# Contrast adjustment on one core: 64 KB rows in three buffers, and all transfers on SyncE's queue

## The chip, the cores and the metric

The kernel runs on one core of one Trainium2 chip. The core has a matrix engine (TensorE, PE in the profile), a vector engine (VectorE, DVE), a scalar engine (ScalarE, ACT), GpSimd (POOL) and SyncE (SP), which here only issues transfers. 16 DMA engines move the data between the chip's memory (HBM) and the on-chip buffer with its 128 partitions. Transfers are put into queues by SyncE and by ScalarE; both queues are served by the same 16 DMA engines. The metric is the device time of one execution in microseconds, median of several runs; less is better.

## The reference

```python
x = np.random.rand(16, 3, 512, 512).astype(np.float32)    # 48 planes of 262,144 pixels, 50.3 MB
factor = np.float32(1.5)

mean = np.mean(x, axis=(2, 3), keepdims=True)
return np.clip(mean + factor * (x - mean), 0, 1).astype(np.float32)
```

Every plane needs its mean before one of its pixels can be written. The kernel computes `factor * x + shift` with `shift = (1 - factor) * mean`, and clips the result to 0 and 1. All of `x` is read once and as many bytes are written, 100.66 MB in all.

## The kernel before

A tile is 128 rows of `ROW` = 8192 floats (32 KB), one row to each partition, 4 MB in all. A plane fills 32 rows, so a tile has four planes, and there are 12 tiles. They lie in `ring`, a tile of six buffers; tile `t` uses buffer `t % 6` and is computed in place.

The work on one tile is in `compute` (L81 to L94):

- VectorE sums the first `SUM` = 4352 floats of each row (the `tensor_reduce`, L81), and beside it ScalarE sums the other 3840 (the `activation` with `accum_out`, L84). ScalarE's copy goes to `junk`, which nobody reads.
- Two matrix products (L86 and L87) with `blockw` add the sums over the 32 rows of a plane, multiply by `(1 - factor) / pixels` and give every row its `shift`, in `bias`. The first takes ScalarE's sum, the second VectorE's.
- VectorE multiplies and adds (L91), then clips (L94), over the whole row. Only tile 0 is done in two pieces, 2048 and 6144 floats.
- `store` (L101) writes the result back. It is issued by ScalarE, so it stands in ScalarE's order behind the sum of its own tile and ahead of the sum of the next.

`load` (L76) is issued by SyncE. Before the loop stand five loads: tile 0 in two pieces (1 MB and 3 MB), tile 1, tiles 2 and 3 in one transfer of 8 MB, and tiles 4 and 5 likewise. In the loop, after tile `t`, tile `t + 6` is loaded into the same buffer, so its load waits in SyncE's order until the store of tile `t` has landed. The order of the program is as written (`manual_schedule`); each engine runs its instructions in that order, with semaphores for what depends on another engine. Stores go through ScalarE's queue (q10 in the profile) and loads through SyncE's (q1), so loads and stores can be under way side by side.

`blockw` is set up on GpSimd at the start by five memsets, one over everything (L61) and one for each block (L63).

Of the kernel before, what the change touches and what calls it, by code (L numbers as in the profile page):

```python
# [1 line left out]

# [4 lines left out]


P = 128  # L10
ROW = 8192
BUFS = 6
SHORT = 2048
FIRST = (SHORT, ROW - SHORT)
SUM = 4352


@with_exitstack
def kernel(
    ctx: ExitStack,  # L20
    tc: tile.TileContext,
    x: bass.AP,
    factor: float,
    out: bass.AP,
):

    nc = tc.nc
    f32 = mybir.dt.float32  # L30
    Alu = mybir.AluOpType
    Act = mybir.ActivationFunctionType

    B, C, H, W = x.shape
    n_img, n_pix = B * C, H * W
    ppi = n_pix // ROW
    per_tile = P // ppi
    n_tiles = n_img // per_tile
    assert ppi * ROW == n_pix and per_tile * n_tiles == n_img

    factor = float(factor)
    wconst = (1.0 - factor) / float(n_pix)

    x_f = x.rearrange("b c h w -> (b c h w)")
    out_f = out.rearrange("b c h w -> (b c h w)")

    def dram(ap, t, c0=0, c1=ROW):
        return bass.AP(tensor=ap.tensor, offset=t * P * ROW + c0, ap=[[ROW, P], [1, c1 - c0]])

    consts = ctx.enter_context(tc.tile_pool(name="consts", bufs=1))  # L50
    xpool = ctx.enter_context(tc.tile_pool(name="xpool", bufs=1))
    small = ctx.enter_context(tc.tile_pool(name="small", bufs=1))
    psum = ctx.enter_context(tc.tile_pool(name="psum", bufs=1, space=bass.MemoryType.PSUM))


    sums = small.tile([P, 2 * n_tiles], f32, name="sums")
    junk = small.tile([P, ROW - SUM], f32, name="junk")
    bias = psum.tile([P, n_tiles], f32, name="bias")

    blockw = consts.tile([P, P], f32, name="blockw")  # L60
    nc.gpsimd.memset(blockw, 0.0)  # L61
    for a in range(0, P, ppi):
        nc.gpsimd.memset(blockw[a : a + ppi, a : a + ppi], wconst)  # L63


    ring = xpool.tile([P, BUFS, ROW], f32, name="ring")

    def load(t, c0=0, c1=ROW, n=1):

        b = t % BUFS  # L70
        src = bass.AP(
            tensor=x_f.tensor,
            offset=t * P * ROW + c0,
            ap=[[ROW, P], [P * ROW, n], [1, c1 - c0]],
        )
        nc.sync.dma_start(out=ring[:, b : b + n, c0:c1], in_=src)  # L76

    def compute(t):
        xt = ring[:, t % BUFS, :]
        own = sums[:, 2 * t : 2 * t + 2]  # L80
        nc.vector.tensor_reduce(  # L81
            out=own[:, 0:1], in_=xt[:, 0:SUM], axis=mybir.AxisListType.X, op=Alu.add
        )
        nc.scalar.activation(out=junk, in_=xt[:, SUM:ROW], func=Act.Copy, accum_out=own[:, 1:2])  # L84
        shift = bias[:, t : t + 1]
        nc.tensor.matmul(shift, blockw, own[:, 1:2], start=True, stop=False)  # L86
        nc.tensor.matmul(shift, blockw, own[:, 0:1], start=False, stop=True)  # L87
        c = 0
        for n in FIRST if t == 0 else [ROW]:
            part = xt[:, c : c + n]  # L90
            nc.vector.tensor_scalar(  # L91
                out=part, in0=part, scalar1=factor, scalar2=shift, op0=Alu.mult, op1=Alu.add
            )
            nc.vector.tensor_scalar(  # L94
                out=part, in0=part, scalar1=0.0, scalar2=1.0, op0=Alu.max, op1=Alu.min
            )
            store(t, c, c + n)
            c += n

    def store(t, c0, c1):  # L100
        nc.scalar.dma_start(out=dram(out_f, t, c0, c1), in_=ring[:, t % BUFS, c0:c1])  # L101

    with tc.manual_schedule():
        load(0, c1=SHORT)
        load(0, c0=SHORT)
        load(1)
        load(2, n=2)
        load(4, n=2)
        for t in range(n_tiles):
            compute(t)  # L110
            if t + BUFS < n_tiles:
                load(t + BUFS)


# [1 line left out]
_INS = ['x', 'factor']  # L116
_OUTS = [((16, 3, 512, 512), 'float32')]

_NUMBERS = {'factor': 1.5}


# [26 lines left out]
```

## Time and profile before

| | before |
|---|---|
| median of 3 runs (lowest to highest) | 239.11 us (239.05 to 239.17) |
| span of the profiled execution, first to last instruction | 237.3 us |
| bytes moved, mean rate over the span | 100.66 MB, 424 GB/s |
| VectorE busy | 163.1 us |
| ScalarE busy | 43.2 us |
| TensorE busy | 14.1 us |
| GpSimd busy | 0.9 us |
| packets of all DMA queues | 3712 |

The profile is of one execution, and its own time is known only as this span. The span begins at the first instruction and ends at the last, and the measured time of a run has a little more around it. Shares are shares of the span. A line such as "L81 DVE ..." is a group of instructions from one line of the kernel on one engine, with its count, busy time and mean. "DMA share" is the mean busy share of the 16 DMA engines. A packet is what a DMA engine moves in one go; here it is one row of a transfer, or the semaphore write that closes a transfer on an engine. A packet counts where it starts, so in short windows the rates waver.

### The profile page before, as it was taken

How to read it: one execution, taken by the hardware profiler on the slowest of the kernel's cores; microseconds unless marked ns; L12 is line 12 of the kernel's file. 1: busy time of each engine (PE TensorE's matmuls, PEld its weight loads, DVE VectorE, ACT ScalarE, POOL GpSimd, SP SyncE). 2: the span in 40 equal slices, each digit the busy share in tenths (PEclk: the TensorE clock that was granted, in tenths of full speed). 3: DMA queues.
4: the chain of work that ended last, by engine and by line, in shares of the span. 5: the costliest groups of instructions: out<-in, count | busy, mean ns of one | idle time of the engine just before them, and what ended most of it. 6: DMA issues, size and time to landing. Idle time of an engine off the chain costs nothing.

```text
span 237.3 us, 285 instructions
## 1 busy us (share of the span) xinstructions
PE 14.1 (6%) x48; PEld 12.0 (5%) x48; DVE 163.1 (69%) x38; ACT 43.2 (18%) x25; POOL 0.9 (0%) x9
## 2 busy tenths in 40 slices
PE   0010010001010001010010100100100100010000
PEld 0010010001010001010010100100100100010000
DVE  0079989048989328999989898891892795687000
ACT  2050230041050023050320504101400500500000
POOL 1000000000000000000000000000000000000000
DMA  7999999999999999999999999999999999999996
GB/s 297 410 442 442 421 442 359 456 439 441 442 436 414 403 431 442 442 442 442 436 442 436 414 409 425 442 442 442 442 436 442 436 420 403 425 442 442 442 442 265
DMA packets 3712, 100.66 MB, mean 424 GB/s; under 512 B 384, under 2 KB 384, under 8 KB 384
## 3 DMA queue, kind: packets, MB, share of 16 engines
q1 hardware_dynamic: 1840, 50.33, 49.7%
q10 hardware_dynamic: 1872, 50.33, 49.2%
HBM read 50.33 MB, written 50.33 MB: 424 GB/s over the span
## 4 chain that ended last, share of the span: by engine, by line
DMA 57%; DVE 29%; another core or an unknown queue 3%; PE 1%; SPq 1%; issue 0%; DVEq 0%
DMA ring<-in_x_dram 41%; DMA out_dram<-ring 16%; DVE sums L81 10%; DVE ring L91 9%; DVE ring L94 9%; PE bias L87 1%; SPq L76 1%; DVEq L91 0%
## 5 line engine op out<-in xcount | busy, mean ns | idle before, releaser
L81 DVE TENSOR_REDUCE sums<-ring 128x1 f32<-128x4352 f32 x12 | 56.2, 4683 | 45.7 <-DMA ring<-in_x_dram 45.7
L84 ACT ACTIVATE junk<-ring 128x3840 f32<-128x3840 f32 x12 | 40.8, 3403 | 163.3 <-DMA ring<-in_x_dram 107.5
L91 DVE TENSOR_SCALAR ring<-ring,bias 128x8192 f32<-128x8192 f32 (+2 forms) x13 | 54.1, 4163 | 8.9 <-PE bias L87 7.4
L94 DVE TENSOR_SCALAR ring<-ring 128x8192 f32<-128x8192 f32 (+2 forms) x13 | 53.3, 4099 | 0.4
L86 PE MATMUL bias<-sums,blockw 128*128 128x1 f32 x24 | 7.0, 361 | 190.8 <-ACT junk L84 190.8
L86 PEld LDWEIGHTS bias<-sums,blockw 128*128 128x128 f32 x24 | 6.0, 312 | 191.7 <-ACT junk L84 175.2
L87 PE MATMUL bias<-sums,blockw 128*128 128x1 f32 x24 | 7.0, 363 | 4.3 <-DVE sums L81 3.9
L87 PEld LDWEIGHTS bias<-sums,blockw 128*128 128x128 f32 x24 | 6.0, 311 | 5.3 <-DVE sums L81 5.0
L84 ACT ACTIVATION_READ_ACCUMULATOR junk<-ring 128x1 f32 x12 | 2.2, 186 | 0.0
L84 ACT ACT_TABLE_LOAD x1 | 1.3, 1283 | 0.7 <-PEq L129 0.7
L63 POOL MEMSET blockw<- 32x32 f32 x4 | 0.5, 117 | 0.2
L61 POOL MEMSET blockw<- 128x128 f32 x1 | 0.2, 204 | 0.3 <-POOLq L129 0.3
L129 POOL MEMSET const-bfloat16-1.0<- 128x1 bf16 x1 | 0.1, 111 | 0.0
L129 POOL MEMSET const-uint8-127<- 128x1 uint8 x1 | 0.1, 111 | 0.0
L129 POOL MEMSET const-float32-1.0<- 128x1 f32 x1 | 0.1, 108 | 0.0
L129 POOL MEMSET const-float32-0.0<- 128x1 f32 x1 | 0.1, 103 | 0.2 <-issue 0.2
## 6 DMA issues: line engine op xcount, KB each, us to landing
out_dram<-ring ACTq DMA_DIRECT2D x11, 4096.0 KB, 35.8
ring<-in_x_dram SPq DMA_DIRECT2D x7, 4096.0 KB, 49.7
ring<-in_x_dram SPq DMA_DIRECT2D x2, 8192.0 KB, 66.7
ring<-in_x_dram SPq DMA_DIRECT2D x1, 3072.0 KB, 11.7
out_dram<-ring ACTq DMA_DIRECT2D x1, 3072.0 KB, 28.2
ring<-in_x_dram SPq DMA_DIRECT2D x1, 1024.0 KB, 4.8
out_dram<-ring ACTq DMA_DIRECT2D x1, 1024.0 KB, 17.5
```

Of the source, the lines that this page charges most:

```text
L61: nc.gpsimd.memset(blockw, 0.0)
L63: nc.gpsimd.memset(blockw[a : a + ppi, a : a + ppi], wconst)
L76: nc.sync.dma_start(out=ring[:, b : b + n, c0:c1], in_=src)
L81: nc.vector.tensor_reduce(out=own[:, 0:1], in_=xt[:, 0:SUM], axis=mybir.AxisListType.X, op=Alu.add)
L84: nc.scalar.activation(out=junk, in_=xt[:, SUM:ROW], func=Act.Copy, accum_out=own[:, 1:2])
L86: nc.tensor.matmul(shift, blockw, own[:, 1:2], start=True, stop=False)
L87: nc.tensor.matmul(shift, blockw, own[:, 0:1], start=False, stop=True)
L91: nc.vector.tensor_scalar(out=part, in0=part, scalar1=factor, scalar2=shift, op0=Alu.mult, op1=Alu.add)
L94: nc.vector.tensor_scalar(out=part, in0=part, scalar1=0.0, scalar2=1.0, op0=Alu.max, op1=Alu.min)
L129: nc = _bacc.Bacc("TRN2", target_bir_lowering=False, num_devices=1)
```

## The change

`ROW` becomes 16,384 floats (64 KB), and `ring` has three buffers in place of six, which is the same size. A tile is now 8 MB and eight planes of 16 rows; there are six tiles. For each tile there are now two sums on VectorE and two on ScalarE (one of each for each half of the row), and four matrix products, the last of which takes VectorE's second sum. Multiply-add and clip run over 16,384 floats at a time, except in the last tile, which is done in two halves.

All transfers are issued by SyncE. The order is written out: loads of tile 0 (two pieces, 1 MB and 7 MB), 1 and 2; stores of 0 and 1; loads of 3 and 4; stores of 2 and 3; load of 5 in two halves; stores of 4 and of the two halves of 5. The waits follow from the three buffers: tile 3 takes the buffer of tile 0, tile 4 that of 1, tile 5 that of 2. `blockw` is filled by one memset and cut to its blocks by two `affine_select`.

```diff
-ROW = 8192
-BUFS = 6
+ROW = 16384
+HALF = ROW // 2
+BUFS = 3
 SHORT = 2048
-FIRST = (SHORT, ROW - SHORT)
 SUM = 4352
...
-    nc.gpsimd.memset(blockw, 0.0)
-    for a in range(0, P, ppi):
-        nc.gpsimd.memset(blockw[a : a + ppi, a : a + ppi], wconst)
+    blocks = blockw.rearrange("p (a b) -> p a b", b=ppi)
+    nc.gpsimd.memset(blockw, wconst)
+    for base, step in ((0, -ppi), (ppi - 1, ppi)):
+        nc.gpsimd.affine_select(
+            out=blocks, in_=blocks, compare_op=Alu.is_ge, fill=0.0, base=base,
+            pattern=[[step, per_tile], [0, ppi]],
+            channel_multiplier=1 if step < 0 else -1,
+        )
...
-        nc.sync.dma_start(out=ring[:, b : b + n, c0:c1], in_=src)
+    def load(t, c0=0, c1=ROW):
+        nc.sync.dma_start(out=ring[:, t % BUFS, c0:c1], in_=dram(x_f, t, c0, c1))
 
+    def store(t, c0=0, c1=ROW):
+        nc.sync.dma_start(out=dram(out_f, t, c0, c1), in_=ring[:, t % BUFS, c0:c1])
 
-    def compute(t):
+    def compute(t, *cuts):
         xt = ring[:, t % BUFS, :]
-        own = sums[:, 2 * t : 2 * t + 2]
-        nc.vector.tensor_reduce(
-            out=own[:, 0:1], in_=xt[:, 0:SUM], axis=mybir.AxisListType.X, op=Alu.add
-        )
-        nc.scalar.activation(out=junk, in_=xt[:, SUM:ROW], func=Act.Copy, accum_out=own[:, 1:2])
+        own = sums[:, 4 * t : 4 * t + 4]
         shift = bias[:, t : t + 1]
-        nc.tensor.matmul(shift, blockw, own[:, 1:2], start=True, stop=False)
-        nc.tensor.matmul(shift, blockw, own[:, 0:1], start=False, stop=True)
-        c = 0
-        for n in FIRST if t == 0 else [ROW]:
-            part = xt[:, c : c + n]
+        for h in range(2):
+            c = h * HALF
+            nc.vector.tensor_reduce(out=own[:, 2 * h : 2 * h + 1], in_=xt[:, c : c + SUM], ...)
+            nc.scalar.activation(
+                out=junk, in_=xt[:, c + SUM : c + HALF], func=Act.Copy,
+                accum_out=own[:, 2 * h + 1 : 2 * h + 2],
+            )
+        for k in (0, 1, 3, 2):
+            nc.tensor.matmul(shift, blockw, own[:, k : k + 1], start=k == 0, stop=k == 2)
+        for c0, c1 in zip((0, *cuts), (*cuts, ROW)):
+            part = xt[:, c0:c1]
             nc.vector.tensor_scalar(
                 out=part, in0=part, scalar1=factor, scalar2=shift, op0=Alu.mult, op1=Alu.add
             )
             nc.vector.tensor_scalar(
                 out=part, in0=part, scalar1=0.0, scalar2=1.0, op0=Alu.max, op1=Alu.min
             )
-            store(t, c, c + n)
-            c += n
+            store(t, c0, c1)
-
-    def store(t, c0, c1):
-        nc.scalar.dma_start(out=dram(out_f, t, c0, c1), in_=ring[:, t % BUFS, c0:c1])
...
-        load(0, c1=SHORT)
-        load(0, c0=SHORT)
+        load(0, 0, SHORT)
+        load(0, SHORT, ROW)
         load(1)
-        load(2, n=2)
-        load(4, n=2)
-        for t in range(n_tiles):
-            compute(t)
-            if t + BUFS < n_tiles:
-                load(t + BUFS)
+        load(2)
+        compute(0)
+        compute(1)
+        load(3)
+        load(4)
+        compute(2)
+        compute(3)
+        load(5, 0, HALF)
+        load(5, HALF, ROW)
+        compute(4)
+        compute(5, HALF)
```

More of the change, by code (lines that the diff above doesn't have):

```diff
@@ L53 @@
     psum = ctx.enter_context(tc.tile_pool(name="psum", bufs=1, space=bass.MemoryType.PSUM))
-    sums = small.tile([P, 2 * n_tiles], f32, name="sums")
-    junk = small.tile([P, ROW - SUM], f32, name="junk")
+    sums = small.tile([P, 4 * n_tiles], f32, name="sums")
+    junk = small.tile([P, HALF - SUM], f32, name="junk")
     bias = psum.tile([P, n_tiles], f32, name="bias")
     blockw = consts.tile([P, P], f32, name="blockw")
-    nc.gpsimd.memset(blockw, 0.0)
-    for a in range(0, P, ppi):
-        nc.gpsimd.memset(blockw[a : a + ppi, a : a + ppi], wconst)
@@ L66 @@
-    ring = xpool.tile([P, BUFS, ROW], f32, name="ring")
[L68 to L74, printed above, removed]
-        )
-        nc.sync.dma_start(out=ring[:, b : b + n, c0:c1], in_=src)
-    def compute(t):
-        xt = ring[:, t % BUFS, :]
-        own = sums[:, 2 * t : 2 * t + 2]
-        nc.vector.tensor_reduce(
-            out=own[:, 0:1], in_=xt[:, 0:SUM], axis=mybir.AxisListType.X, op=Alu.add
-        )
-        nc.scalar.activation(out=junk, in_=xt[:, SUM:ROW], func=Act.Copy, accum_out=own[:, 1:2])
-        shift = bias[:, t : t + 1]
-        nc.tensor.matmul(shift, blockw, own[:, 1:2], start=True, stop=False)
-        nc.tensor.matmul(shift, blockw, own[:, 0:1], start=False, stop=True)
-        c = 0
-        for n in FIRST if t == 0 else [ROW]:
-            part = xt[:, c : c + n]
+    blocks = blockw.rearrange("p (a b) -> p a b", b=ppi)
@@ new lines @@
+    nc.gpsimd.memset(blockw, wconst)
+    for base, step in ((0, -ppi), (ppi - 1, ppi)):
+        nc.gpsimd.affine_select(
+            out=blocks,
+            in_=blocks,
+            compare_op=Alu.is_ge,
+            fill=0.0,
+            base=base,
+            pattern=[[step, per_tile], [0, ppi]],
+            channel_multiplier=1 if step < 0 else -1,
+        )
+    ring = xpool.tile([P, BUFS, ROW], f32, name="ring")
+    def load(t, c0=0, c1=ROW):
+        nc.sync.dma_start(out=ring[:, t % BUFS, c0:c1], in_=dram(x_f, t, c0, c1))
@@ new lines, in store @@
+    def store(t, c0=0, c1=ROW):
+        nc.sync.dma_start(out=dram(out_f, t, c0, c1), in_=ring[:, t % BUFS, c0:c1])
+    def compute(t, *cuts):
+        xt = ring[:, t % BUFS, :]
+        own = sums[:, 4 * t : 4 * t + 4]
+        shift = bias[:, t : t + 1]
+        for h in range(2):
+            c = h * HALF
+            nc.vector.tensor_reduce(
+                out=own[:, 2 * h : 2 * h + 1],
+                in_=xt[:, c : c + SUM],
+                axis=mybir.AxisListType.X,
+                op=Alu.add,
+            )
+            nc.scalar.activation(
+                out=junk,
+                in_=xt[:, c + SUM : c + HALF],
+                func=Act.Copy,
+                accum_out=own[:, 2 * h + 1 : 2 * h + 2],
+            )
+        for k in (0, 1, 3, 2):
+            nc.tensor.matmul(shift, blockw, own[:, k : k + 1], start=k == 0, stop=k == 2)
+        for c0, c1 in zip((0, *cuts), (*cuts, ROW)):
+            part = xt[:, c0:c1]
```

## The prediction

> **What bounds the kernel now.** I read the page first (busy shares, slices, queues), then a table of windows, then the DMA view of one steady stretch, and last the trace's records of single DMA packets. From the page:
>
> ```profile
> span 237.3 us, 285 instructions
> PE 14.1 (6%) x48; PEld 12.0 (5%) x48; DVE 163.1 (69%) x38; ACT 43.2 (18%) x25; POOL 0.9 (0%) x9
> DMA  7999999999999999999999999999999999999996
> q1 hardware_dynamic: 1840, 50.33, 49.7%
> q10 hardware_dynamic: 1872, 50.33, 49.2%
> ```
>
> VectorE, the busiest engine, works 69% of the span. The 16 DMA engines are busy in every slice, and the two queues' shares add to 98.9%: 234.7 us of 237.3. The kernel is bound by DMA from the first load to the last store, so only packets that are fewer or shorter, or stretches in which packets run slow, can give time; a hole in the queue costs its whole length. The windows say where the rate is below its best (columns: stretch, length, busy time by engine, clock, DMA share, GB/s):
>
> ```profile
> 13.00:22.00 9.00, 1.15 (x4) 1.01 (x4) 8.28 (x4) 3.38 (x2) 0.00 (x0) 1.00 1.06 459
> 22.00:42.00 20.00, 1.18 (x4) 1.00 (x4) 19.08 (x5) 3.50 (x2) 0.00 (x0) 1.00 0.99 410
> 60.00:100.00 40.00, 2.35 (x8) 2.00 (x8) 30.18 (x8) 6.99 (x4) 0.00 (x0) 1.00 1.01 435
> 140.00:200.00 60.00, 3.52 (x12) 3.00 (x12) 45.62 (x11) 10.49 (x6) 0.00 (x0) 1.00 1.00 434
> 218.00:235.00 17.00, 0.00 (x0) 0.00 (x0) 0.14 (x1) 0.00 (x0) 0.00 (x0) 1.00 1.00 432
> ```
>
> Loads and stores mixed run at 434 to 435 GB/s; stores alone, on one queue (the last stretch), at 432; loads alone at 459, where the window's edges count whole packets. So the rate depends neither on direction nor on the number of queues. Only 22 to 42 us, where the stores begin beside the loads, is slower. The steady stretch 100 to 200 us gives the price of a packet:
>
> ```profile
> DMA packets 1485, 43.42 MB, mean 434 GB/s; under 512 B 160, under 2 KB 160, under 8 KB 160
> q1 hardware_dynamic: 748, 21.89, 50.7%
> q10 hardware_dynamic: 737, 21.53, 49.9%
> ```
>
> 1325 packets are rows of 32 KB (160 are the 4-byte semaphore writes, 16 for each transfer). 100.6% of 100 us on 16 engines is 1610 us, or 1.215 us a row. The single records say the same: a row of 8 KB takes 309 ns, of 24 KB 912 ns, of 32 KB 1213 ns, a semaphore write 9 ns. The three rows lie on a line: 7.8 ns fixed plus 36.78 ns per 1000 bytes.
>
> **The sum for the kernel before, to check the method.** Each engine moves 8 of a transfer's 128 rows. Per direction: 8 x (309 + 912 + 11 x 1213) = 116.5 us; both 233.02. 24 transfers x 9 ns = 0.22. Packets longer than their kind: 0.49 us per engine at the start (first loads, 1.7 to 4 us), 0.27 at 22.8 to 32 us (the first store begins), 0.52 at 35 to 45 us (the second begins). The first packet starts at 1.74. Together 236.26; the span is 237.27, so 1.0 us is the lag of the slowest engine, the last landing and the closing instructions. The median of the runs, 239.11, is 1.84 above this execution's span; I carry both over.
>
> **The change, part by part.** *Rows of 64 KB.* If a row is one packet, the line gives 7.8 + 65,536 x 0.03678 = 2418 ns against 2 x 1213 = 2426. A row of 56 KB gives 2117. Loads: 8 x (309 + 2117 + 4 x 2418 + 2 x 1213) = 116.19 us; stores: 8 x (5 x 2418 + 2 x 1213) = 116.13. Sum 232.32, so -0.70. Bounds: -0.70 as one packet, 0 if cut into 32 KB, and +1.5% (+3.4 us) if cut into 8 KB (4 x 309 = 1236 against 1213); I take -0.70, as all three sizes of before run as whole rows.
>
> The Trainium skill (DMA: Bandwidth & Descriptors, Latency and other measured facts) warns against power-of-two row pitches in HBM: 207 GB/s per direction at a 512 KiB pitch, 103 at 4 MiB. This change doubles the pitch from 32 to 64 KB, still below the first of these, so by the page nothing is lost; halving the rate would add some 230 us. No run here shows it yet.
>
> *Fewer transfers.* 15 for 24: nine semaphore packets less per engine, -0.08 us. In the stores-only tail one transfer follows another on the same queue at 432 GB/s, so a transfer's boundary costs nothing else.
>
> The same page (Anatomy of one DMA) fits a transfer, on GpSimd's path, as about 2.0 us plus its bytes at 436 GB/s; nine transfers fewer would then be worth 18 us. The trace disagrees for queued transfers: 9 ns of engine time each.
>
> *One queue.* Nothing alternates any more: the order is L0 (in two), L1, L2, S0, S1, L3, L4, S2, S3, L5 (in two halves), S4, S5 (in two halves). That takes away the two starts of stores beside loads (0.27 and 0.52 us above), and puts five changes of direction into one queue, which before has none. What one costs is not in the trace. Nearest rows: from 60 us on, loads and stores alternate on each engine packet by packet and every packet takes its 1213 ns, so 0; at the second store's start the neighbours are stretched by 0.52; a queue that drained fully would lose landing plus first packet, 0.37 + 1.0 (issue at 0.74, packet at 1.74) = 1.4 us. I take 0 for four and 0.27 for the first, because steady alternation is nearest; against before that is -0.52. Both ends stay for the range: -0.79 with none, +6.2 with five drains.
>
> *Does the queue ever run dry?* SyncE now issues everything and waits in order. Stream, in us: L0 ends at 1.74 + 0.49 + 19.4 = 21.6, L1 41.0, L2 60.3, S0 79.7, S1 99.0, L3 118, L4 138, S2 157, S3 176, L5 186 and 196, S4 215, S5 225 and 234.5; landing is seen some 0.8 later. VectorE needs for a tile: two reductions 2 x 4.68; 0.74 for the shift; multiply-add of 16,384 at 0.521 ns an element (from 1.29, 3.42 and 4.49 us for 2048, 6144 and 8192) 8.76; clip 8.70: 27.6 us. Stores are ready: S0 22.4 + 27.6 = 50.0 (needed 60.3), S1 77.6 (needed 79.7), S2 105.2 (138), S3 118.9 + 27.6 = 146.5 (157), S4 174 (196), S5a 196.6 + 4.7 + 0.7 + 8.9 = 210.9 (215), S5b 219.9 (225). Loads: L3 waits at the head of SP for S0 to land (80.5) while S1 runs until 99; L4 waits for S1 (99.8) while L3 runs; L5 waits for S2 (158) while S3 runs, and S4 is queued behind it. All are covered; without cover each would cost about 1.4 us. The thin one is S1: 2.1 us ahead. Issue to first packet was 1.0 us on the idle queue and 3.7 for the first store beside busy loads (20.91 to 24.64), so a hole of up to 1.6 us; I take 0, by the row of 1.0, because no second queue stands in S1's way.
>
> *The rest.* ScalarE loses its 13 DMA issues of 0.34 us and keeps its 12 sums; it had waited 163 us. VectorE's element count is unchanged. PE has the same 24 matrix products, of which the last again waits for the last reduction (0.74). GpSimd builds the weights with two selects instead of four memsets (0.58 us); the select is not in the trace, but the first product comes at about 27 us instead of 16.5, so it has 25 us of cover, and past that would first eat S1's 2.1 us. All nothing.
>
> Sum: -0.70 - 0.08 - 0.52 = -1.30, a span of 235.97 and a time of 237.8 us.
>
> **The rivals.** *Rows cut into 32 KB* (the change is then not what it says of its rows): -0.70 is gone, 239.11 - 0.60 = 238.5. For: no packet above 32 KB in the trace. Against: three sizes, all whole.
>
> *Changes of direction cost on one queue* (slower): at each of L2-S0, S1-L3, L4-S2, S3-L5, L5-S4 the engine stretches packets as at the second store's start. At 0.52 each: 5 x 0.52 - 0.79 - 0.78 = +1.03, 240.1 us; at a full drain of 1.4, 244.5. From 0.41 us each it decides for slower by over 0.2%. For: 22 to 42 us is the slowest window, and it holds the stores' start. Against: the steady stretches.
>
> *S1 comes late*: a hole at 80 us of up to 1.6: 237.8 + 1.6 = 239.4, no change; the compute of two large tiles in series (55.2 us against 57.3 of the queue) is what speaks for it.
>
> **How the numbers follow.** A measurement of this kernel can tell about 0.2%, 0.5 us. Chances: forecast 0.5, rows cut 0.13 (on the edge, half faster, half the same), direction 0.22, S1 late 0.12 (a part of the hole leaves it faster, the whole the same), anything else 0.03. Faster 0.60, same 0.14, slower 0.26. The range: below, the start's 0.49 and the 0.27 could go too, 237.0; above, direction changes at 0.6 each, 240.5; the likeliest case's own range is 237.3 to 238.5.
>
> **What would show it.** Packets: 2160 in all against 3712 (1920 rows, 15 x 16 semaphore writes); 3440 if long rows are cut into two. GB/s at 434 in every slice after the first, no dip at 60, 99, 138, 176 and 196 us. S1's first packet right behind S0's last near 80. The last load landed at about 196 us, the last store issued at 220. Wrong would be: dips at those times (direction), DMA share below 98.5% with a hole near 80 (S1), or a packet of 64 KB taking more than 2.43 us.

## The result and the profile after

| | before | changed |
|---|---|---|
| median of 10 runs each (lowest to highest) | 239.14 us (239.04 to 239.32) | 239.79 us (239.16 to 240.15) |
| ratio, 95% interval | | 1.0023 [1.0014, 1.0032] |
| profiled execution: time / span | - / 237.3 us | 239.56 / 237.8 us |

The changed kernel is slower by 0.65 us in the medians; by the ratio it is 0.23%, with an interval that leaves out no change. The forecast was faster by 1.3 us. The time lies inside the stated range, but on the other side of no change.

The page of the changed kernel, the lines that answer to those of before:

```profile
span 237.8 us, 235 instructions
PE 12.6 (5%) x48; PEld 11.4 (5%) x48; DVE 160.5 (67%) x26; ACT 43.2 (18%) x25; POOL 1.1 (0%) x7
DMA  8997989899889898989898998989899999989996
DMA packets 2160, 100.66 MB, mean 423 GB/s; under 512 B 240, under 2 KB 240, under 8 KB 240
q1 hardware_dynamic: 2160, 100.66, 98.6%
```

Still bound by DMA: 98.6% of the span against 98.9%. There are 2160 packets, as forecast for whole rows of 64 KB. Where the time went is seen when the windows are cut at the ends of transfers, so that each holds one transfer of 8 MB (stretch, length, busy times, clock, DMA share, GB/s). L1 is here the load of tile 1 and S0 the store of tile 0; in a line of the profile such as "ACT L95", L95 is a line of the kernel. The changed kernel, from L1 to L3:

```profile
21.60:40.95 19.35, 2.16 (x8) 1.93 (x8) 17.54 (x3) 6.99 (x4) 0.00 (x0) 1.00 1.00 434
40.95:61.65 20.70, 2.03 (x8) 1.85 (x8) 19.92 (x5) 6.99 (x4) 0.00 (x0) 1.00 1.00 405
61.65:81.00 19.35, 0.00 (x0) 0.00 (x0) 19.32 (x3) 6.99 (x4) 0.00 (x0) 1.00 1.00 434
81.00:100.65 19.65, 2.03 (x8) 1.86 (x8) 18.86 (x4) 0.00 (x0) 0.00 (x0) 1.00 1.08 467
100.65:119.65 19.00, 0.00 (x0) 0.00 (x0) 4.37 (x1) 0.00 (x0) 0.00 (x0) 1.00 0.92 400
```

L1 takes 19.35 us and S0 takes 19.35 us. L2, between them, takes 20.70 us: 1.35 us more, with the engines busy all the time (share 1.00). S1 and L3 together are as long as two of the others (38.65 us); what S1 seems to lose, L3 gets back (by the landings, averaged over the engines, S1 takes 19.77 us and L3 18.91). So one stage is long, the last load ahead of the first store. The single records say which packets it is: of L2, the last packet of each engine before S0 took 3.40 to 3.72 us instead of 2.418, 1.13 us more in the mean over the 16 engines; another 0.25 us per engine lies on L2's packets between 41 and 51 us. The same is seen in ScalarE's starts, which wait for the loads of tiles 0, 1 and 2 (timeline: start, duration):

```profile
22.59 3.40 ACT L95 ACTIVATE junk<-ring 128x3840 f32<-128x3840 f32 x1 [20.51 <-DMA ring<-in_x_dram]
42.00 3.40 ACT L95 ACTIVATE junk<-ring 128x3840 f32<-128x3840 f32 x1 [12.39 <-DMA ring<-in_x_dram]
62.64 3.40 ACT L95 ACTIVATE junk<-ring 128x3840 f32<-128x3840 f32 x1 [13.62 <-DMA ring<-in_x_dram]
```

Tile 1 comes 19.4 us after tile 0, tile 2 comes 20.6 us after tile 1. At the next change from loads to stores (L4 to S2, 137 us) the packets are 0.23 us longer, at the third (L5 to S4, 196 us) 0.03. At the changes from stores to loads nothing is lost. All that packets took beyond what is usual for their size adds to 1.27 us per engine in the kernel before and to 2.09 in the changed one: +0.82.

The other half of the sum is what the rows should have brought. The kernel before, its last three stores of 4 MB, alone on their queue:

```profile
206.40:216.05 9.65, 1.18 (x4) 1.01 (x4) 8.88 (x3) 0.91 (x2) 0.00 (x0) 1.00 1.01 435
216.05:225.75 9.70, 0.00 (x0) 0.00 (x0) 2.09 (x1) 0.00 (x0) 0.00 (x0) 1.00 1.00 432
225.75:235.40 9.65, 0.00 (x0) 0.00 (x0) 0.00 (x0) 0.00 (x0) 0.00 (x0) 1.00 1.01 435
```

9.65 to 9.70 us for 4 MB is 19.3 to 19.4 us for 8 MB: the pace that the changed kernel has with rows twice as long. By the landings, averaged over the engines, it is 9.67 to 9.68 us and 19.34 us.

### The profile page after: what moved, and what is told of

It reads as the page before. It is cut to its first block, busy times and chain, and to the rows that moved or that the text cites. A ratio compares the mean times of both kernels' runs of the same rounds, so it can differ in the third digit from the quotient of the medians.

```text
span 237.8 us, 235 instructions
## 1 busy us (share of the span) xinstructions
PE 12.6 (5%) x48; PEld 11.4 (5%) x48; DVE 160.5 (67%) x26; ACT 43.2 (18%) x25; POOL 1.1 (0%) x7
## 2 busy tenths in 40 slices
DMA packets 2160, 100.66 MB, mean 423 GB/s; under 512 B 240, under 2 KB 240, under 8 KB 240
## 3 DMA queue, kind: packets, MB, share of 16 engines
q1 hardware_dynamic: 2160, 100.66, 98.6%
## 4 chain that ended last, share of the span: by engine, by line
DMA 55%; DVE 32%; another core or an unknown queue 5%; PE 1%; SPq 0%; issue 0%; DVEq 0%
DMA ring<-in_x_dram 41%; DMA out_dram<-ring 13%; DVE ring L105 11%; DVE ring L108 11%; DVE sums L89 10%; PE bias L102 1%; SPq L78 0%; SPq L81 0%; DVEq L105 0%; DVEq L89 0%
## 5 line engine op out<-in xcount | busy, mean ns | idle before, releaser
L95 ACT ACTIVATE junk<-ring 128x3840 f32<-128x3840 f32 x12 | 40.8, 3403 | 157.8 <-DMA ring<-in_x_dram 157.7
L105 DVE TENSOR_SCALAR ring<-ring,bias 128x16384 f32<-128x16384 f32 (+1 forms) x7 | 52.8, 7538 | 4.5 <-PE bias L102 4.5
L108 DVE TENSOR_SCALAR ring<-ring 128x16384 f32<-128x16384 f32 (+1 forms) x7 | 52.3, 7475 | 0.2
L102 PE MATMUL bias<-sums,blockw 128*128 128x1 f32 x48 | 12.6, 358 | 191.0 <-DVE sums L89 180.8
L102 PEld LDWEIGHTS bias<-sums,blockw 128*128 128x128 f32 x48 | 11.4, 320 | 192.2 <-DVE sums L89 154.3
L95 ACT ACTIVATION_READ_ACCUMULATOR junk<-ring 128x1 f32 x12 | 2.2, 186 | 0.0
L64 POOL TENSOR_SCALAR_AFFINE_SELECT blockw<-blockw 128x128 f32<-128x128 f32 x2 | 0.7, 343 | 0.1
```

The costliest lines, as they stand in the source:

```text
L64: nc.gpsimd.affine_select(out=blocks, in_=blocks, compare_op=Alu.is_ge, fill=0.0, base=base, pattern=[[step, per_tile], [0, ppi]], channel ...
L95: nc.scalar.activation(out=junk, in_=xt[:, c + SUM : c + HALF], func=Act.Copy, accum_out=own[:, 2 * h + 1 : 2 * h + 2],)
L102: nc.tensor.matmul(shift, blockw, own[:, k : k + 1], start=k == 0, stop=k == 2)
L105: nc.vector.tensor_scalar(out=part, in0=part, scalar1=factor, scalar2=shift, op0=Alu.mult, op1=Alu.add)
L108: nc.vector.tensor_scalar(out=part, in0=part, scalar1=0.0, scalar2=1.0, op0=Alu.max, op1=Alu.min)
```

## The experiments

The theory behind them: the stretch before S0 is the price of the first large store, paid once, and rows of 64 KB are worth nearly nothing. The rivals: the turn of a queue from loads to stores costs it each time; VectorE and ScalarE are in the way at 58 us; the row size matters in the stretch; it is the chip that was used. "Stretch" below is always the sum of what packets took beyond the median time of packets of their size, per engine, from the trace's packet records.

**A small store ahead of all others** (two kernels). 32 KB of zeros into the head of tile 0's output, once through ScalarE's queue at the start and once in SyncE's queue behind the first load:

```diff
+    warm = small.tile([P, 64], f32, name="warm")
+    nc.gpsimd.memset(warm, 0.0)
...
+        nc.scalar.dma_start(out=dram(out_f, 0, 0, 64), in_=warm)    # warm_act
         load(0, 0, SHORT)
+        nc.sync.dma_start(out=dram(out_f, 0, 0, 64), in_=warm)      # warm_sp
         load(0, SHORT, ROW)
```

> The changed kernel with one small store added: 128 rows of 256 B from a tile of zeros into the head of tile 0's output, issued by ScalarE at the very start (tile 0's own store overwrites it later). Theory 'first store': the 1.13 us per engine at the change from L2 to S0 is paid once, by whichever store is first on the DMA engines. Then the packets at 58 us go back to within 0.25 us of 2.418 us, the time falls by about 0.9 us from 239.8 to 238.9. Rival 'turn of the queue': the one queue pays when a long run of loads turns into stores; the stretch at 58 us stays near 1.1 us and the time at 239.8 (ratio 1.002 to 1.003 to before).

> The same small store, but on SyncE's queue between the two loads of tile 0, so that it stands in the line of loads. 'First store': the cost moves to about 5 us, into the same line, and the time stays near 239.8, with at most 0.25 us left at 58 us. 'Turn of the queue': a short turn at 5 us costs little and the stretch at 58 us stays near 1.1 us; time 239.8 to 240.1.

Measured: through ScalarE 239.60 us, ratio 1.0013 [1.0001, 1.0026], and the stretch at 58 us is 1.41 us. A first store packet is not what costs. The other one took 241.44 us, ratio 1.0087 [1.0074, 1.0100], which neither theory had. Its stretch at 58 us is 0.64 us in the mean, between what the two theories expected; another 0.74 us lies on packets from 4 to 56 us, where the changed kernel has 0.27. Whether the small store moved a part of the price there stays open. Its landings tell where the time went: from the load of tile 0 on, two of the 16 engines are behind. Fourteen engines land that load between 22.26 and 22.70 us, the other two at 23.55 and 23.56. At the last store it is 236.07 to 237.07 us for fourteen and 238.81 and 238.84 for two, a spread of 2.77 us, where the changed kernel has 0.77. The mean over the engines at the end is 236.73 us against 236.52. So nearly all of the loss there is two late engines, for which the end waits.

**Rows cut in the access pattern.** Each 64 KB row written as two pieces of 32 KB that adjoin in memory (the side of the buffer is split in the same way, which the cut below leaves out):

```diff
-        return bass.AP(tensor=ap.tensor, offset=t * P * ROW + c0, ap=[[ROW, P], [1, c1 - c0]])
+        return bass.AP(tensor=ap.tensor, offset=t * P * ROW + c0,
+                       ap=[[ROW, P], [HALF, 2], [1, HALF]] if c1 - c0 == ROW else [[ROW, P], [1, c1 - c0]])
```

> The changed kernel with every 64 KB row written as two pieces of 32 KB in the transfers' access pattern; order, queue and buffers unchanged. If packets follow the pieces: 32 KB packets of 1.213 us, 0.58 us more over the nine whole-tile transfers (9 x 8 x 2 x 1.213 - 9 x 8 x 2.418), so 240.4; the stretch at 58 us, if it is a time for each engine and not a share of a packet, stays near 1.1 us. If packets are joined again nothing changes: 239.8.

Measured: 239.58 us, ratio 1.0019 [1.0006, 1.0032], with 2160 packets, 1152 of them of 64 KB: the pieces were joined, and this run is a repeat of the changed kernel. As such it is of use: its stretch at 58 us is 1.49 us.

**Stores on their own queue again**, with the large rows and three buffers:

```diff
     def store(t, c0=0, c1=ROW):
-        nc.sync.dma_start(out=dram(out_f, t, c0, c1), in_=ring[:, t % BUFS, c0:c1])
+        nc.scalar.dma_start(out=dram(out_f, t, c0, c1), in_=ring[:, t % BUFS, c0:c1])
```

> The changed kernel with its stores issued by ScalarE, on its own queue, as in the kernel before; rows of 64 KB and three buffers stay. Loads and stores are then under way side by side from 50 us on. 'Turn of the queue': no turn is left, the stretch goes, the 64 KB packets' -0.7 us remains: 238.4 to 238.7. 'First store': the cost stays wherever the first store starts, 0.8 to 1.1 us, at about 52 us: 239.2 to 239.8.

Measured: 252.54 us in the median of six runs (245.58 to 253.87). Both expectations miss the time. Windows of its profiled execution (253.25 us, span 251.5 us; same columns):

```profile
200.00:216.00 16.00, 0.00 (x0) 0.00 (x0) 0.62 (x1) 0.56 (x1) 0.00 (x0) 1.00 1.00 432
216.00:230.50 14.50, 1.17 (x4) 1.00 (x4) 13.73 (x4) 2.93 (x2) 0.00 (x0) 1.00 0.02 9
230.50:251.00 20.50, 0.00 (x0) 0.00 (x0) 8.08 (x2) 0.00 (x0) 0.00 (x0) 1.00 0.95 409
```

For 14.5 us the DMA has nothing to do (share 0.02) while VectorE works on the last tile. With two queues the last load shares the engines with the stores. Fourteen engines have landed it by 207.7 us, instead of 198, and two only at 214.3 and 215.4; by then almost no store is left to run beside the last tile's compute. The two late engines alone are 7.7 us of the wait. The fastest run, 245.58 us, is 7.7 us below the profiled one, which would fit a run without them, but it has no profile; it is still 6.3 us above the kernel before. In the written order of the one queue, L5 stands ahead of S4, whose 19.35 us cover that compute. So with tiles of 8 MB the one queue served this order better than two; another order for two queues was not tried. The stretch at the first store is there too, 1.51 us at 53 us, on load packets that end where the first store packet starts (56.9 us), though the queue of the loads never turns: the cost is not the turn of a queue.

**The changed order and queue with the rows of before.** A transfer is two times 128 rows of 32 KB that do not adjoin; a plane lies in 32 rows again, and each half of a tile has its own shift:

```diff
-    ppi = n_pix // ROW
+    ppi = n_pix // HALF
...
-        return bass.AP(tensor=ap.tensor, offset=t * P * ROW + c0, ap=[[ROW, P], [1, c1 - c0]])
+        h, c = divmod(c0, HALF)
+        n = (c1 - c0) // HALF
+        inner = [[1, c1 - c0]] if n < 2 else [[P * HALF, n], [1, HALF]]
+        return bass.AP(tensor=ap.tensor, offset=(2 * t + h) * P * HALF + c, ap=[[HALF, P], *inner])
...
-        load(0, SHORT, ROW)
+        load(0, SHORT, HALF)
+        load(0, HALF, ROW)
```

> The changed kernel's order, queue and 8 MB transfers, with the rows of before: a transfer is two times 128 rows of 32 KB that do not adjoin, each plane lies in 32 rows again, and each half of a tile has its own shift. By the prediction's price (2418 ns against 2 x 1213) the loss is 0.70 us: 240.3 to 240.5. By the pace from landing to landing (stores alone in the kernel before: 9.67 us for 4 MB; in the changed one: 19.34 us for 8 MB) the row's size is worth nothing: 239.6 to 239.8, within 0.1% of the changed kernel.

Measured: 239.61 us, ratio 1.0015 [1.0007, 1.0024], against 1.0023, 1.0019 and 1.0016 for the changed kernel and its two repeats. The 0.7 us of the prediction are not there. Windows of this kernel, L2 and S0:

```profile
41.10:61.20 20.10, 2.02 (x8) 1.85 (x8) 19.35 (x5) 6.99 (x4) 0.00 (x0) 1.00 1.01 416
61.20:80.60 19.40, 1.44 (x6) 1.35 (x6) 19.37 (x4) 6.99 (x4) 0.00 (x0) 1.00 1.00 432
```

S0 takes 19.40 us in windows cut to 0.05 us; by the landings 19.37 against 19.34. That is 0.03 us for 8 MB and some 0.3 us over the nine transfers of whole tiles that have 64 KB rows in the changed kernel. L2 is long here too, by 0.70 us; the stretch before S0 is 0.84 us by the records. The three profiles of the changed program have 1.13, 1.49 and 1.51 there, so the row size may matter in the stretch; one profile does not settle it.

**The first store in two pieces, the last load in two pieces, or both.**

```diff
-        load(2)                               # l2_small, turn_small
+        load(2, 0, ROW - SHORT)
+        load(2, ROW - SHORT, ROW)
-        compute(0)                            # cut0, turn_small
+        compute(0, SHORT)
```

> The changed kernel with tile 0's result stored in two pieces, 2048 floats of each row first (1 MB) and the other 14,336 after them. If the loss at the first store grows with the size of the packets that start there (8 KB rows in the kernel before: 0.27 us, then 24 KB rows: 0.52), the stretch before S0 falls from 1.1 to 1.5 us to 0.3, with up to 0.5 at the second piece: 239.0 to 239.4. If it is a fixed price of the first bulk store, it stays: 239.6 to 239.8.

> The changed kernel with L2, the last load ahead of the first store, in two transfers: 14,336 floats of each row, then 2048 (8 KB rows). The stretch so far always fell on the last load packet of each engine before the first bulk store (1.1 to 1.5 us with 64 KB rows, 0.84 with 32 KB rows). 'It goes by the load packet in flight': with 8 KB packets there it falls to 0.3 or less, and the time to 238.6 to 238.9, below the kernel before. 'A fixed price of the first bulk store': it only falls on another packet, and the time stays at 239.5 to 239.8.

> Both sides of the first change small: L2's last piece as in the run with the split L2, and tile 0 stored as 2048 and then 14,336 floats of each row. 'By the packets in flight on both sides': stretch 0.3 or less, 238.6 to 238.9, even if the split of L2 alone does nothing. 'Fixed price': 239.5 to 239.8.

Measured: store cut 239.58 us, 1.0017 [1.0007, 1.0027], stretch 1.27 us; load cut 239.89, 1.0024 [1.0015, 1.0033], stretch 1.40; both 239.90, 1.0036 [1.0023, 1.0050], stretch 1.30. With 8 KB rows as the last load, five or six of an engine's eight last packets are longer, most by 0.1 to 0.4 us, and the sum is as large as it was on one packet of 64 KB. The price does not go by the packet in flight. The small packets also show when it is paid (load cut): 8 KB packets that start between 58.1 and 61.1 us take mostly 0.45 to 0.65 us; from 61.5 us on they take their usual 0.31 again, and the first store packet starts at 61.8. So loads run slowly for some 3 us shortly before the first store packet.

**Transfers alone.** The compute is left out, and what is stored is the input: in the order of the changed kernel, in an order with five turns from loads to stores (the expectation counts six), and with 1 MB stored early:

```diff
 copy_same:   L0 (1+7 MB) L1 L2 S0 S1 L3 L4 S2 S3 L5 (4+4) S4 S5 (4+4)
 copy_turns:  L0 (1+7 MB) L1 S0 L2 S1 L3 S2 L4 S3 L5 S4 S5 (4+4)
 copy_early:  L0 (1+7 MB) S0 (1 MB) L1 L2 S0 (7 MB) S1 L3 L4 S2 S3 L5 (4+4) S4 S5 (4+4)
```

> Only the transfers of the changed kernel, in the same order, on the same queue; sums, products, multiply-add and clip are left out, so that what is stored is the input. 'Compute in the way': the stretch of 1.1 to 1.5 us at the first change from loads to stores comes from VectorE and ScalarE working on the buffer at 58 us; without them it goes, and the time is about 238.2. 'First bulk store': it is a matter of the DMA alone and stays above 1 us; time 239.3 to 239.8, as nothing else is on the path.

> Only transfers again (what is stored is the input), but in the order L0 L1 S0 L2 S1 L3 S2 L4 S3 L5 S4 S5: six changes from loads to stores in place of three. 'First bulk store': one stretch of 1.1 to 1.5 us at 41 us, a small one (0.2 to 0.5) at the next, none after; 239.3 to 240. 'Every change pays': about 1.1 us at each of six, 243 or more. 'Compute in the way': none at all, 238.2.

> Only transfers (what is stored is the input), with a 1 MB store (8 KB rows of tile 0) between the loads of tile 0 and tile 1, and the rest of tile 0 where its store stood. 'First bulk store': 1 MB is bulk enough; the price moves to 21 us (up to 1.5 us there) and the change at 60 us costs 0.2 to 0.35 like all later ones. Rival 'each large store after a long run of loads until some megabytes have been written': 0.3 at 21 us and still about 1 us at 60 us. Time 239.5 to 240 by both.

Measured, one run each: 239.83, 241.16 and 240.80 us. In the first the stretch before S0 is 1.45 us with no other engine at work: the compute is not in the way. In the second it is 1.49 us at the first turn (L1 to S0, at 41 us) and 0.18 to 0.34 at the other four. The windows of the third, from the 7 MB of tile 0 to the 7 MB of S0 (columns: stretch, length, GpSimd, clock, DMA share, GB/s):

```profile
4.45:23.05 18.60, 0.00 (x0) 1.00 1.01 398
23.05:25.80 2.75, 0.00 (x0) 1.00 1.27 542
25.80:44.85 19.05, 0.00 (x0) 1.00 0.96 417
44.85:64.20 19.35, 0.00 (x0) 1.00 1.01 436
64.20:81.10 16.90, 0.00 (x0) 1.00 0.99 431
```

7 MB take 16.90 us in the last line and 18.60 us in the first, just ahead of the early store; by the records the stretch there is 1.72 us. L2 (44.85 to 64.20) now takes its usual 19.35 us, and the stretch at its end is 0.07 us. So the large price is paid once, at the first store of a megabyte or more, and it moves with that store; the turn from L4 to S2 costs 0.54 us here, as much as any later turn cost in these runs. 32 KB through ScalarE's queue were not enough to pay it (1.41 us were left).

The times of the last two are longer for another reason as well: at the end the engines are 2.04 and 1.62 us apart, against 0.77 us in the changed kernel.

**The first store of the kernel before in one piece.**

```diff
-        for n in FIRST if t == 0 else [ROW]:
+        for n in [ROW]:
```

> The kernel before, with tile 0's result stored in one piece of 4 MB instead of 1 MB and 3 MB; everything else is unchanged. 'Fixed price of the first bulk store, by row size': one stretch of about 0.8 us at the first store (some 39 us) in place of 0.27 and 0.52; time within 0.1% of before, 239.0 to 239.5. 'The split keeps it small': 1.1 us or more, 239.5 to 239.9.

Measured: 240.57 us, ratio 1.0050 [1.0031, 1.0068]. The stretch at the first store is 1.08 us in place of 0.27 and 0.52, on packets of loads just as there. It falls unevenly: three engines have packets stretched by 1.7 to 1.8 us, are behind by some 0.9 us at the next load's landing, and the landings are 1.58 us apart at the end instead of 0.60. With the 1 MB piece first the kernel before pays less, 0.79 us; of the 1.14 us by which the last landing is later here than there, 0.55 us are in the mean over the engines, and the rest is the late ones.

**That gentle start for the changed kernel**, with rows of 64 KB and of 32 KB (there tile 0 is stored in three pieces, 1, 3 and 4 MB), and the changed kernel beside them:

```diff
-        compute(0)
+        compute(0, SHORT)
...
-            store(t, c0, c1)
+            if t == 0 and c0 == 0:
+                nc.scalar.dma_start(out=dram(out_f, t, c0, c1), in_=ring[:, t % BUFS, c0:c1])
+            else:
+                store(t, c0, c1)
```

> The changed kernel with the first 1 MB of tile 0's result (2048 floats of each row) stored through ScalarE's queue as soon as it is clipped, beside the loads; everything else, the other 7 MB of tile 0 too, stays on SyncE's queue. This is how the kernel before starts to store. 'Abrupt or gentle': the first bulk store costs 1.1 to 1.7 us when all engines turn to it at once, and 0.7 to 0.8 when 8 KB rows of it alternate with loads; then about 0.3 us at 36 to 50 us and at most 0.5 at 60 us are left, and the time is 238.9 to 239.3. 'Fixed price': 1.1 us or more in all, 239.6 to 239.8.

> The same gentle start on the kernel with 32 KB rows (the changed order, queue and 8 MB transfers, rows as before). 'Abrupt or gentle': 238.8 to 239.2, and equal to the kernel before within 0.15%. 'Fixed price': 239.5 to 239.7, as without it.

> The changed kernel itself once more, beside the two with the gentle start on the same chip: 239.6 to 239.9, and 1.1 to 1.5 us of stretch at the first change from loads to stores. If it were as fast as the gentle ones here, their difference would be the chip's.

Measured on one chip:

| | median (lowest to highest) | ratio to before | stretch at the first stores |
|---|---|---|---|
| before | 239.33 (238.93 to 239.74) | | 0.27 + 0.52 (first profile) |
| again: the changed kernel | 239.70 (239.33 to 240.44) | 1.0016 [1.0007, 1.0025] | 1.51 |
| gentle, 64 KB rows | 238.92 (238.76 to 241.75) | 1.0004 [0.9980, 1.0027] | 0.71 + 0.23 |
| gentle, 32 KB rows | 239.43 (239.29 to 239.96) | 1.0006 [0.9997, 1.0015] | 0.37 + 0.42 |

L1, L2 and the 7 MB of S0 in the kernel with the gentle start and 64 KB rows (the store of 1 MB runs beside L1 and L2):

```profile
21.50:42.00 20.50, 2.16 (x8) 1.93 (x8) 18.90 (x5) 7.00 (x4) 0.00 (x0) 1.00 1.00 418
42.00:63.50 21.50, 2.03 (x8) 1.85 (x8) 20.72 (x5) 7.00 (x4) 0.00 (x0) 1.00 1.01 431
63.50:80.45 16.95, 0.00 (x0) 0.00 (x0) 16.91 (x3) 7.00 (x4) 0.00 (x0) 1.00 1.00 433
```

S0 ends at 80.45 here and at 81.00 in the changed kernel. The stretch is 0.94 us in all, more than the 0.7 to 0.8 expected (0.71 us where the 1 MB starts, and not 0.3), but less than the 1.51 of the changed kernel beside it on the same chip. The stretch is not one chip's: one-queue runs with 64 KB rows on three chips have 1.27 to 1.51 us at that place. Nine of the twelve runs are at 238.76 to 239.25 us, below the median of the kernel before; three are at 240.70 to 241.75. No profile shows those three. The interval holds both signs, so whether this version beats the kernel before is not settled. With 32 KB rows the time, 239.43, is above the expected 239.2, and equal to before within 0.15%, as was expected. Its stretch, 0.79 us, is hardly below the 0.84 of the same rows without the gentle start. So a gentle start made the stretch smaller with 64 KB rows, by one profile against three, and not clearly with 32 KB rows.

## Why the prediction was wrong, point by point

**Rows of 64 KB, -0.70 us.** Right that a row is one packet, and right to the nanosecond that it takes 2418 ns. Wrong is the step from there to a sum. In the records each packet of an engine starts 3 to 4 ns before the end of the one ahead, for both sizes, so the difference of two durations (8 ns for 64 KB) is no difference of pace: about half of it is left. The prediction's sum for the kernel before could not show this. It was too long by some 0.8 us (232 packets for an engine), and what then remained to the span was put down to the end. The pace from landing to landing was in the trace of before as well: 9.67 us for 4 MB, which is 8 x 1.209 us, not 8 x 1.213. Landings price 64 KB against 32 KB rows at about 0.3 us in all (the kernel with the rows of before), and the times show no difference that can be told. One bound in this part is also added up wrongly: rows cut into 8 KB would be 768 rows of 309 ns for an engine, 237.3 us, so 4.3 us more and not 3.4. Nothing hung on it.

**Fewer transfers, -0.08 us.** The semaphore packets lie in the same overlap; 9.67 to 9.68 us from landing to landing, for eight rows of 1.209 us and the semaphore packet, leave next to nothing for this term. The 2 us for a transfer that the prediction weighed and refused are not seen either.

**One queue, -0.52 us.** This term decided the sign. It took the two stretches at 22 to 45 us for a cost of stores that start beside loads, which one queue would save. They are what the first bulk store costs, and a store has to be first in any order. That it goes with the first bulk store is shown by the transfers alone, where it moved with that store to 20 us and left its old place; that it is not a queue's turn, by the two queues. The price was 0.79 us in the kernel before and 1.1 to 1.5 us in the changed kernel and its repeats. Why it is larger there is not shown: the stores begin with all engines at once and not with 8 KB rows between loads, and the rows are larger; the kernels with a gentle start and with 32 KB rows fit either. With what the second turn and L2's own packets lose, all longer packets came to +0.82 us against before instead of -0.52 (2.09 us in all; 2.20 and 2.11 in the two repeats). That is 1.34 us of the 1.9 us between the forecast and the spans.

The sum with the measured terms: +0.82 from longer packets, +0.07 because the first packet starts at 1.81 us instead of 1.74, and between -0.3 us and nothing from the rows, gives +0.6 to +0.9; the spans differ by 0.57 us and the medians by 0.65.

**The queue never runs dry: right.** S0 was issued at 50.2 us (forecast 50.0), S1 at 77.6 (77.6), S2 at 105.05 (105.2); S0 ran until 81 and S1 came right behind it. From S3 on the stores are ready 1.6 to 1.8 us later than forecast, most of it the stretch before S0. The select on GpSimd took 0.34 us twice, far from the path.

**The rivals.** Rows cut in two: no. S1 late: no. Changes of direction at 0.52 us on each of five: the place was right for the first (L2 to S0), but the price is 1.13, 0 (S1 to L3), 0.23, 0 and 0.03 us, so it is mainly a price of the first store and not of each change. That this rival's time, 240.1 us, came nearer to 239.79 than the forecast is luck: it added 0.52 us at five places. The named sign, dips in the rate at 60, 99, 138, 176 and 196 us, came only at the first. Of the row pitch that the Trainium skill warns about (DMA: Bandwidth & Descriptors, Latency and other measured facts) no loss is seen at 64 KB: L1 runs at 434 GB/s. The page's smallest pitch is 512 KiB; that nothing is lost at 64 KB was the prediction's inference, and this run bears it out.

## What to carry to other kernels

Price a DMA-bound kernel by the pace from landing to landing over whole transfers, and not by the durations of single packets: of a difference of 8 ns between packet sizes the overlap left half here. A stretch that shows once, at the first of something, need not be saved by another order; look whether the new order makes that first step harder. Where all engines share the work, read the landing of the last engine too: a change that costs the mean little can leave one or two engines behind, and the end waits for them.

## What the runs showed of the hardware that was not expected

- The first store of 1 MB or more costs the DMA engines 0.8 to 1.7 us in the mean, once. It lies on load packets shortly before the first store packet, of 8 to 64 KB, with and without compute, on one queue or two. A store of 32 KB through ScalarE's queue ahead of it did not take the price over (1.41 us left); in SyncE's queue 0.64 us were left; one of 1 MB took it over (0.07 us left). Where 8 KB rows of the first store alternate with loads from another queue it is 0.8 to 0.9 us in all. What in the chip is behind it stays open.
- Turns from stores to loads in one queue cost nothing in the changed kernel and at most 0.16 us in any run (both sides of the first change small, 178 us); later turns from loads to stores 0 to 0.54 us.
- Single engines can fall behind early and stay behind: two of the 16 with the small store in SyncE's queue, up to 2.77 us at the end, where the mean engine lost 0.2 us, and two with the stores on their own queue, 7.7 us at the last load. What makes them fall behind was not tried.
- Two adjoining pieces of 32 KB in an access pattern were moved as one packet of 64 KB.
